# Single-precision 128-point transforms in a bidirectional Hyena and neighbourhood-attention encoder layer

## The chip, the core and the metric

The kernel runs on one NeuronCore of one Trainium2 chip. The core has a matrix engine (TensorE; PE in the profile, with its weight loads as PEld), a vector engine (VectorE, DVE), a scalar engine (ScalarE, ACT), a general engine (GpSimd, POOL) and SyncE (SP), whose queue issues all of this kernel's DMAs. PE reads its operands from the on-chip memory SBUF and adds into the eight banks of PSUM. Each engine works through its own instructions in a fixed order and waits for the others by semaphores. The metric is the time of one execution on the device, in microseconds.

## The reference, cut to what matters

One layer is computed for two sequences, a prompt of 1024 tokens ("p") and a sample of 512 ("s"), of width 1024. Half of the width goes through a Hyena branch, a long convolution by FFT with a filter that a small network makes; the other half goes through attention in windows of a 2-D grid.

```python
h = rmsnorm(x, norm_g);  z = h @ w_in
hy_in = short_conv(hy_in, conv_w, conv_b);  x0, x1, vv = split(hy_in)
kfilt = hyena_filter(L, ...)                       # length 2 L
U = rfft(x1 * vv, n=2 * L);  K = rfft(kfilt, n=2 * L)
y = irfft(U * K, n=2 * L)[:L] + (x1 * vv) * bias
y_hy  = rmsnorm(x0 * y) * silu(hy_gate)
y_att = rmsnorm(neighbourhood_attention(q, k, v, rpb)) * silu(att_gate)
out = x + concat([y_hy, y_att]) @ w_out
```

## The kernel before

**Three products for one.** A float32 product is split: an operand is rounded to fp32r (hi) and the rest kept as a second fp32r tile (lo), and hi*hi + hi*lo + lo*hi are added in PSUM. Projections (L392 and L405), attention and output (L1111) work so, and so do the 128-point transforms. The halves of a weight are made by a cast on ACT or DVE (L365) and a subtraction on POOL (L366).

**The transforms.** A sequence of 2L points is split into classes. DVE makes each class's z, a [128, 2, 128] tile with real and imaginary part (zc), by 8- or 16-point butterflies. Then comes a 128-point transform across the partitions, which is a product with a cosine and a sine matrix of the class. Class 0 holds two real classes and is "packed" (matrices fc); all others are "generic" (matrices dftm). The prompt has 8 classes for each block of 128 channels, the sample has 4, and both have 4 blocks.

In `fwd_generic` ACT casts z into Z (hi, L449), POOL subtracts (lo, L450), and ACT writes the negated copies (L451), so that one row of products serves both parts. `mm3` (L461 to L463) then issues three matmuls of 256 columns for the cosine and three for the sine. `fwd_packed` does the same without the negated copy (L469, L470).

In the filters (`k_phase`, `k_block`) ACT scales the result into Kw, which goes to DRAM. In the convolution (`long_conv`) DVE multiplies the spectrum by the filter's (Kc, from DRAM) into yA and yB, sums them into yA, and ACT, POOL and ACT make Y out of it (L665 to L667) for the inverse transform by `mm3`; ACT copies the result into W, and DVE does the inverse butterflies. The packed class goes through Ybd (L649, L650).

**Constants.** `dft_mats` loads the class matrices as hi and lo, for the filters in one transfer (km), for the prompt's and the sample's convolution each in three, through the room of tiles that are needed later (W, xu, s4). ACT casts them into dftm (L429).

**Stages.** In the first 95 us the prompt's x is normed, turned and split, the filters' network runs, and the first projections start. From 95 to 310 us the filters' transforms alternate with q, k and v of the prompt; from 310 to 575 us there is the prompt's hyena; from 575 to 925 us the prompt's attention runs together with the projections and the hyena of the sample; after that come the outputs and the sample's attention.

**What sets the order.** Generators of each stage are woven in the turns that a plan counts out, with priorities. The framework then lays each engine's instructions in a fixed order from these priorities and an estimate of durations, and waits for a free buffer where a pool has none. `nz`, `nZ`, `nY` and `nK` are the numbers of buffers of z, Z, Y and Kc; yA and yB have nz - 1. The banks for transforms (tag a) are three in the filters, four with b in the prompt's hyena, and one in the sample's.

## Time and profile before

| | |
|---|---|
| Median of 3 runs | 1100.7 us (1096.19 to 1102.8) |
| Span of the profiled execution | 1101.3 us, 18549 instructions |
| PE matmul busy | 1030.7 us (94%), 6492 instructions |
| PE weight loads busy | 895.6 us (81%) |
| DVE busy | 824.4 us (75%), 2098 instructions |
| ACT busy | 561.1 us (51%), 1223 instructions |
| POOL busy | 539.9 us (49%), 480 instructions |
| DMA | 154.87 MB, 141 GB/s over the span |

The profile is one execution, and its own time is its span. Busy shares are means over stages with different limits. A matmul's record covers its whole way through the array, so records of consecutive matmuls overlap, and the price of one is read from the distance of starts. A wait is put down to the semaphore that came last.

### The profile page before, as it was taken

The page shows a single profiled execution, that of the slowest core. Times are in us where ns is not written, and L with a number is a line of the kernel's source. Part 1 is how long each engine was busy: PE and PEld are TensorE (multiplying, and loading weights), DVE is VectorE, ACT ScalarE, POOL GpSimd, SP SyncE. Part 2 cuts the span into 40 slices and gives each one's busy share as a digit, 9 for nine tenths or more (in the row PEclk, how much of TensorE's full clock was granted, in tenths as well). Part 3 has the DMA queues.
Part 4 walks back from the last instruction along what each step waited for, and adds up shares of the span by engine and source line. Part 5 has one row for each costly group of instructions (what it writes and reads, how often), then busy time and mean ns, then how long its engine had stood idle before and what let it go on. Part 6 is the DMA issues. An engine that isn't in the chain of part 4 may idle for free. (4 is left out here: it accounts for less than half of the span.)

```text
span 1101.3 us, 18549 instructions
## 1 busy us (share of the span) xinstructions
PE 1030.7 (94%) x6492; PEld 895.6 (81%) x6492; DVE 824.4 (75%) x2098; ACT 561.1 (51%) x1223; POOL 539.9 (49%) x480
## 2 busy tenths in 40 slices
PE   3999898998999999999898999999999999899998
PEld 2888887987888878787786887888777798798898
DVE  5988679456148597868768898999886868966874
ACT  6644616444534343443425577667567764564530
POOL 2133636325245474545445645455455564766452
PEclk9999999899999999999999899999999999999999
DMA  9134461645612121122375244445544376966522
GB/s 343 34 122 144 143 207 61 219 150 164 224 39 74 46 79 54 50 72 77 118 227 173 78 129 146 120 141 182 140 129 138 114 243 190 321 203 205 164 76 89
DMA packets 110780, 154.87 MB, mean 141 GB/s; under 512 B 7793, under 2 KB 80315, under 8 KB 109919
## 3 DMA queue, kind: packets, MB, share of 16 engines
q1 hardware_dynamic: 110687, 153.69, 44.3%
q8 instruction: 51, 0.84, 0.3%
q14 instruction: 42, 0.34, 0.1%
HBM read 110.35 MB, written 43.32 MB: 140 GB/s over the span
## 5 line engine op out<-in xcount | busy, mean ns | idle before, releaser
L366 POOL TENSOR_TENSOR wlo<-wraw,whi 128x512 fp32r<-128x512 f32 x160 | 231.5, 1451 | 308.4 <-ACT whi L365 180.7
L392 PE MATMUL bank<-hThi_p,whi 128*128 128x512 f32 x320 | 125.2, 391 | 2.0 <-DVE cx L75 2.0
L392 PE MATMUL bank<-hTlo_p,whi 128*128 128x512 f32 x320 | 125.5, 392 | 0.0
L392 PE MATMUL bank<-hThi_p,wlo 128*128 128x512 f32 x320 | 125.4, 392 | 0.0
L405 PE MATMUL bank<-whi,hThi_p 128*128 128x256 f32 x384 | 110.4, 290 | 2.5 <-ACT qsq L849 2.0
L1111 PE MATMUL bank<-whi,hi 128*128 128x256 f32 x384 | 111.0, 291 | 0.8 <-ACT hi L1090 0.5
L405 PE MATMUL bank<-wlo,hThi_p 128*128 128x256 f32 x384 | 110.8, 291 | 0.0
L1111 PE MATMUL bank<-wlo,hi 128*128 128x256 f32 x384 | 110.0, 288 | 0.0
L1111 PE MATMUL bank<-whi,lo 128*128 128x256 f32 x384 | 109.5, 289 | 0.3 <-POOL lo L63 0.3
L405 PE MATMUL bank<-whi,hTlo_p 128*128 128x256 f32 x384 | 108.1, 289 | 0.0
L450 POOL TENSOR_TENSOR Z<-zc,Z 128x256 fp32r<-128x256 f32 x80 | 69.5, 878 | 49.2 <-ACT Z L449 36.2
L1002 ACT ACTIVATE s_sb<-s_sb,mx 128x360 f32<-128x360 f32 (+1 forms) x96 | 60.4, 629 | 63.6 <-DVE mx L998 63.0
L405 PEld LDWEIGHTS bank<-whi,hThi_p 128*128 128x128 f32 x384 | 74.2, 194 | 4.9 <-ACT qsq L849 2.4
L1111 PEld LDWEIGHTS bank<-whi,hi 128*128 128x128 f32 x384 | 73.4, 191 | 4.1 <-issue 2.1
L405 PEld LDWEIGHTS bank<-wlo,hThi_p 128*128 128x128 f32 x384 | 74.5, 194 | 1.6 <-issue 0.7
L1111 PEld LDWEIGHTS bank<-wlo,hi 128*128 128x128 f32 x384 | 73.6, 192 | 1.6 <-issue 1.6
L1111 PEld LDWEIGHTS bank<-whi,lo 128*128 128x128 f32 x384 | 73.1, 192 | 1.7 <-issue 1.1
L405 PEld LDWEIGHTS bank<-whi,hTlo_p 128*128 128x128 f32 x384 | 73.3, 194 | 1.2 <-issue 0.7
L392 PEld LDWEIGHTS bank<-hThi_p,whi 128*128 128x128 f32 x320 | 60.3, 188 | 14.0 <-DVE cx L75 2.4
L392 PEld LDWEIGHTS bank<-hTlo_p,whi 128*128 128x128 f32 x320 | 60.4, 189 | 11.3
L392 PEld LDWEIGHTS bank<-hThi_p,wlo 128*128 128x128 f32 x320 | 60.3, 188 | 11.3
L392 PE MATMUL bank<-hThi_s,whi 128*128 128x512 f32 x160 | 64.6, 407 | 4.4 <-DVE cvv L75 2.3
(292 smaller groups left out, 3108.4 us busy)
## 6 DMA issues: line engine op xcount, KB each, us to landing
wraw<-in_w_ch_dram SPq DMA_DIRECT2D x40, 512.0 KB
wraw<-in_w_tk_dram SPq DMA_DIRECT2D x24, 512.0 KB
wraw<-in_w_out_dram SPq DMA_DIRECT2D x16, 512.0 KB
V<-v_p SPq DMA_DIRECT2D x32, 240.0 KB
v_p<-vg SPq DMA_DIRECT2D x32, 160.0 KB
K_p<-Kw SPq DMA_DIRECT2D x4, 1088.0 KB
x<-in_x_prompt_dram SPq DMA_DIRECT2D x8, 512.0 KB
dec<-in_dec_p_dram SPq DMA_DIRECT2D x16, 256.0 KB
```

The lines of the kernel that those rows point to most:

```text
L366: nc.gpsimd.tensor_tensor(out=lo, in0=r, in1=f32(hi), op=ALU.subtract)
L392: nc.tensor.matmul(ps, lhsT=w, rhs=h[s][:, k], start=(k == 0 and i == 0), stop=(k == KC - 1 and i == 2))
L405: nc.tensor.matmul(pss[t // 2][:, t % 2, :], lhsT=h[t // 4][:, k, t % 4 * P:(t % 4 + 1) * P], rhs=w, start=(k == 0 and i == 0 and t % 2 == ...
L450: nc.gpsimd.tensor_tensor(out=Z[:, 1, 0:2, :], in0=z, in1=f32(Z[:, 0, 0:2, :]), op=ALU.subtract)
L1002: nc.scalar.activation(out=s_sb[:, :n], in_=s_sb[:, :n], func=AF.Exp, bias=mx, scale=-1.0, accum_out=l)
L1111: nc.tensor.matmul(ps[:, j, :], lhsT=h[:, tok], rhs=w, start=(k == 0 and i == 0 and j == 0), stop=(k == 3 and i == 2 and j == 1))
```

## The change

The transforms no longer split their operands. The constants are summed back to single precision (hi + lo, on DVE) when they are loaded, with a third matrix, the negated sine, made by ACT. A generic transform is three matmuls in single precision, straight from zc or yA: one of 256 columns with the cosine and two of 128 columns with the sine and its negative. The packed transform and its inverse are two matmuls of 256 columns each. Z, Y and their conversions on ACT and POOL are gone. Ybd is written by DVE directly, in four half-partition operations instead of two whole ones. The constants come one class at a time, through two tiles in turn (km0, km1 in the filters), four (W, o8, s4, d4) in the prompt's convolution and two (W, s4) in the sample's. In the prompt's hyena `nz` is 8 instead of 4 and `nK` 4 instead of 2. Comments and docstrings were removed as well, so line numbers differ by some 20; they are left out here.

```diff
-        self.fc = g.tile([P, 8, P], F32R, name="fc")
-        m = ["M1f", "M2f", "M1i", "M2i"]
-        self.F = {n: (self.fc[:, 2 * i, :], self.fc[:, 2 * i + 1, :]) for i, n in enumerate(m)}
+        self.fc = g.tile([P, 4, P], F32, name="fc")
+        self.F = {n: self.fc[:, i] for i, n in enumerate(["M1f", "M2f", "M1i", "M2i"])}
...
     def dft_load(self, t, src, pool, tag):
-        r = pool.tile([P, t.shape[1], P], F32, name=tag, bufs=1)
+        r = pool.tile([P, *src.shape[1:]], F32, name=tag, bufs=1)
         self.dma(r, src)
-        self.nc.scalar.copy(out=t, in_=r)
+        self.add(t, r[:, :, 0], r[:, :, 1])
...
     def dft_mats(self, pool, src, fs, stage, tags):
-        t = pool.tile([P, len(fs), 4, P], F32R, name="dftm", bufs=1)
...
+        t = pool.tile([P, len(fs), 3, P], F32, name="dftm", bufs=1)
+        for i, (f, tag) in enumerate(zip(fs, itertools.cycle(tags))):
+            self.dft_load(t[:, i, 0:2], src[:, f - 1].rearrange("p (n a) c -> p n a c", a=2), stage, tag)
+            self.nc.scalar.mul(out=t[:, i, 2], in_=t[:, i, 1], mul=-1.0)
+        return [None] + [tuple(t[:, i, k] for k in range(3)) for i in range(len(fs))]
+    def turn128(self, o, f, z, inverse):
+        c, s, ns = self.dft[f]
+        mm = self.nc.tensor.matmul
+        mm(o, lhsT=c, rhs=z, start=True, stop=False)
+        mm(o[:, 0:P], lhsT=ns if inverse else s, rhs=z[:, 1], start=False, stop=False)
+        mm(o[:, P:], lhsT=s if inverse else ns, rhs=z[:, 0], start=False, stop=True)
...
-    def fwd_generic(self, fp, z, f):
-        Z = fp.tile([P, 2, 3, P], F32R, name="Z", bufs=self.nZ)
-        nc.scalar.copy(out=Z[:, 0, 0:2, :], in_=z)
-        nc.gpsimd.tensor_tensor(out=Z[:, 1, 0:2, :], in0=z, in1=f32(Z[:, 0, 0:2, :]), op=ALU.subtract)
-        nc.scalar.mul(out=Z[:, :, 2, :], in_=f32(Z[:, :, 0, :]), mul=-1.0)
+    def fwd_generic(self, z, f):
         ps = self.bank()
         o = ps[:, 0:256]
-        c, s = self.dft[f]
-        self.mm3(o, c, (Z[:, 0, 0:2, :], Z[:, 1, 0:2, :]), True, False)
-        self.mm3(o, s, (Z[:, 0, 1:3, :], Z[:, 1, 1:3, :]), False, True)
+        self.turn128(o, f, z, False)
...
+    def fwd_packed(self, z):
         ps = self.bank()
-        self.mm3(ps[:, 0:256], self.F["M1f"], (Z[:, 0], Z[:, 1]), True, False)
-        self.mm3(ps[:, 256:512], self.F["M2f"], (Z[:, 0], Z[:, 1]), False, True)
+        for i, n in enumerate(("M1f", "M2f")):
+            self.nc.tensor.matmul(ps[:, i * 256:i * 256 + 256], lhsT=self.F[n], rhs=z, start=i == 0, stop=i == 1)
...
-                self.sub(A[:, 0], A[:, 0], A[:, 1])
-                self.add(A[:, 1], Bt[:, 0], Bt[:, 1])
                 Y = self.Ybd
                 for h in range(2):
                     r = slice(64 * h, 64 * h + 64)
-                    nc.scalar.copy(out=Y[r, 0, :, h, :], in_=A[r])
-                    nc.gpsimd.tensor_tensor(out=Y[r, 1, :, h, :], in0=A[r], in1=f32(Y[r, 0, :, h, :]), op=ALU.subtract)
+                    self.sub(Y[r, 0, h], A[r, 0], A[r, 1])
+                    self.add(Y[r, 1, h], Bt[r, 0], Bt[r, 1])
...
-            Y = fp.tile([P, 2, 3, P], F32R, name="Y", bufs=max(1, self.nY - 1))
-            nc.scalar.copy(out=Y[:, 0, 1:3, :], in_=A)
-            nc.gpsimd.tensor_tensor(out=Y[:, 1, 1:3, :], in0=A, in1=f32(Y[:, 0, 1:3, :]), op=ALU.subtract)
-            nc.scalar.mul(out=Y[:, :, 0, :], in_=f32(Y[:, :, 2, :]), mul=-1.0)
-            c, s = self.dft[f]
-            self.mm3(o, c, (Y[:, 0, 1:3, :], Y[:, 1, 1:3, :]), True, False)
-            self.mm3(o, s, (Y[:, 0, 0:2, :], Y[:, 1, 0:2, :]), False, True)
+            self.turn128(o, f, A, True)
...
-        self.nz, self.nZ, self.nY, self.nK, self.nx, self.nb = 4, 4, 4, 2, 1, 2
-        self.dft = self.dft_mats(fp, self.io["hmat"], range(1, 8), fp, (("W", 4), ("xu", 2), ("s4", 1)))
+        self.nz, self.nZ, self.nY, self.nK, self.nx, self.nb = 8, 4, 4, 4, 1, 2
+        self.dft = self.dft_mats(fp, self.io["hmat"], range(1, 8), fp, ("W", "o8", "s4", "d4"))
...
-        self.dft = self.dft_mats(fp, self.io["hmat"], (2, 4, 6), fp, (("W", 1), ("xu", 1), ("W", 1)))
+        self.dft = self.dft_mats(fp, self.io["hmat"], (2, 4, 6), fp, ("W", "s4"))
```

The framework lays the whole order anew. Three places show how.

On PE, early in the filters, before: the sine products of one class (bank_888) wait for later conversions, so another class and three matmuls of a projection (L405) stand between them.

```order
L461 MATMUL bank_906<-Z_902,dftm_487 128x256
L462 MATMUL bank_888<-Z_884,dftm_487 128x256
L463 MATMUL bank_888<-Z_884,dftm_487 128x256
L405 MATMUL bank_1483<-whi_1181,hThi_p_270 128x256
L405 MATMUL bank_1483<-wlo_1182,hThi_p_270 128x256
L405 MATMUL bank_1483<-whi_1181,hTlo_p_272 128x256
L461 MATMUL bank_888<-Z_884,dftm_487 128x256
L462 MATMUL bank_888<-Z_884,dftm_487 128x256
L463 MATMUL bank_888<-Z_884,dftm_487 128x256
L462 MATMUL bank_906<-Z_902,dftm_487 128x256
L463 MATMUL bank_906<-Z_902,dftm_487 128x256
```

The same place now (L404 is the old L405, L443 to L445 are the three products of `turn128`, L458 the packed one):

```order
L404 MATMUL bank_1037<-whi_1044,hTlo_p_273 128x256
L458 MATMUL bank_891<-zc_888,fc_74 128x256 x2
L443 MATMUL bank_902<-zc_899,dftm_487 128x256
L444 MATMUL bank_902<-zc_899,dftm_487 128x128
L445 MATMUL bank_902<-zc_899,dftm_487 128x128
L443 MATMUL bank_913<-zc_910,dftm_487 128x256
L444 MATMUL bank_913<-zc_910,dftm_487 128x128
L445 MATMUL bank_913<-zc_910,dftm_487 128x128
L404 MATMUL bank_1395<-whi_1146,hThi_p_270 128x256
L404 MATMUL bank_1395<-wlo_1147,hThi_p_270 128x256
```

A class's matmuls now stand together, and read z itself.

On DVE, the same stage, writes of z in the odd classes of the prompt's filters, before, with what they wait for (Pool_49 is POOL's semaphore):

```order
L63 TENSOR_TENSOR zc_952<-oE_946,oO_936 128x256 [waits DVE_49,Pool_49]
L63 TENSOR_TENSOR zc_966<-oE_946,oO_936 128x128 [waits Pool_49]
L63 TENSOR_TENSOR zc_966<-oO_936,oE_946 128x128
L63 TENSOR_TENSOR zc_981<-oE2_947,oO2_937 128x256 [waits DVE_49,Pool_49]
L63 TENSOR_TENSOR zc_995<-oE2_947,oO2_937 128x128 [waits Pool_49]
L63 TENSOR_TENSOR zc_995<-oO2_937,oE2_947 128x128
L850 TENSOR_REDUCE qss8_1282<-qsq_1296 128x8 [waits Activation_49]
```

and now:

```order
L63 TENSOR_TENSOR zc_949<-oE_943,oO_933 128x256 [waits DVE_49,PE_49]
L63 TENSOR_TENSOR zc_956<-oE_943,oO_933 128x128 [waits PE_49]
L63 TENSOR_TENSOR zc_956<-oO_933,oE_943 128x128
L63 TENSOR_TENSOR zc_964<-oE2_944,oO2_934 128x256 [waits DVE_49,PE_49]
L582 MEMSET Kw_879 1x128 [waits Activation_49]
L63 TENSOR_TENSOR oab_1341<-xk_564 128x256 [waits DVE_49]
```

The wait for a free buffer of z moved from POOL to PE; there are 32 such waits for PE at writes of z, all of them in the filters.

Constants of the prompt's convolution, before, on ACT, behind the gates (vg) and ahead of the short convolution (cx1):

```order
L886 ACTIVATE vg_3343<-bank_3318 128x512
L429 CAST dftm_3507<-W_3508 128x2048
L429 CAST dftm_3507<-xu_3511 128x1024
L429 CAST dftm_3507<-s4_3514 128x512
L415 ACTIVATE cx1_3521<-bank_3532,pc_70 128x512
```

and now, on DVE, between the first (vg_2423) and the second half (vg_2750) of v's results (DMAHW are the transfers' semaphores):

```order
L63 TENSOR_TENSOR vg_2423<-bank_2189,vg_2423 128x8x64 [waits DMAHW5_49,DMAHW4_49,DMAHW7_49,DMAHW3_49,Activation_49]
L63 TENSOR_TENSOR dftm_3196<-W_3197 128x256 [waits DMAHW0_49]
L63 TENSOR_TENSOR dftm_3196<-o8_3201 128x256 [waits DMAHW1_49]
L63 TENSOR_TENSOR dftm_3196<-s4_3205 128x256 [waits DMAHW2_49]
L63 TENSOR_TENSOR dftm_3196<-d4_3209 128x256 [waits DMAHW3_49]
L63 TENSOR_TENSOR dftm_3196<-W_3213 128x256 [waits DMAHW0_49]
L63 TENSOR_TENSOR dftm_3196<-o8_3217 128x256 [waits DMAHW1_49]
L63 TENSOR_TENSOR dftm_3196<-s4_3221 128x256 [waits DMAHW2_49]
L63 TENSOR_TENSOR vg_2750<-bank_2534,vg_2750 128x8x64 [waits DMAHW5_49,DMAHW6_49,DMAHW4_49,DMAHW7_49,DVE_49,Activation_49]
```

The load of these constants moved to another engine and ahead of the end of v.

## Rows read from the trace of the kernel before

**Rows 1.** The page's busy shares: us, share of the span, instructions.

```profile
PE 1030.7 (94%) x6492; PEld 895.6 (81%) x6492; DVE 824.4 (75%) x2098; ACT 561.1 (51%) x1223; POOL 539.9 (49%) x480
```

**Rows 2.** Busy us (instructions) by stage: PE, PEld, DVE, ACT, POOL; then clock, DMA.

```profile
95.00:310.00 215.00, 201.39 (x1334) 180.66 (x1333) 127.39 (x348) 99.92 (x253) 94.96 (x86) 0.98 0.48 157
310.00:575.00 265.00, 253.50 (x1341) 215.72 (x1340) 195.33 (x515) 104.76 (x234) 136.80 (x115) 0.98 0.27 85
575.00:925.00 350.00, 336.92 (x2082) 284.11 (x2082) 296.87 (x749) 227.58 (x473) 188.91 (x171) 0.99 0.48 145
```

**Rows 3.** Timeline of PE in the prompt's hyena: start us, us, instruction.

```profile
340.18 0.28 PE L461 MATMUL bank<-Z,dftm 128*128 128x256 f32 x1
...
340.89 0.40 PE L392 MATMUL bank<-hTlo_p,whi 128*128 128x512 f32 x1
```

**Rows 4.** Timeline of PE around a single-precision product of the filters' network.

```profile
52.65 1.02 PE L166 MATMUL bank<-h_s,w 128*128 128x512 f32 x2
53.11 0.68 PE L405 MATMUL bank<-whi,hTlo_p 128*128 128x256 f32 x1
53.63 0.28 PE L405 MATMUL bank<-whi,hThi_p 128*128 128x256 f32 x1
```

**Rows 5.** Chain that ended last: eight single-precision instructions of one column.

```profile
901.76 0.79 PE bank L828 x8
```

**Rows 6.** Costliest groups, conversions: name, forms, count | busy us, mean ns | idle before, releasers.

```profile
L450 POOL TENSOR_TENSOR Z<-zc,Z 128x256 fp32r<-128x256 f32 x80 | 69.5, 878 | 49.2 <-ACT Z L449 36.2 <-issue 6.6 <-DVE vg L63 3.0
...
L451 ACT ACTIVATE Z<-Z 128x256 fp32r<-128x256 f32 x80 | 33.1, 417 | 39.5 <-POOL Z L450 39.2
L449 ACT CAST Z<-zc 128x256 fp32r<-128x256 f32 x80 | 31.2, 403 | 19.7 <-DVE zc L75 7.9 <-DVE zc L63 6.1 <-PE bank L463 3.3
```

**Rows 7.** The same view, matmuls of the transforms, with most idle time before them.

```profile
L462 PE MATMUL bank<-Z,dftm 128*128 128x256 f32 x160 | 46.4, 292 | 4.7 <-POOL Z L450 4.7
L461 PE MATMUL bank<-Z,dftm 128*128 128x256 f32 x160 | 46.2, 291 | 3.3 <-DVE yB L63 1.2 <-ACT Kw L600 0.8 <-ACT Z L451 0.6
...
L461 PE MATMUL bank<-Z,fc 128*128 128x256 f32 x32 | 9.4, 292 | 2.6 <-ACT Z L469 2.6
```

**Rows 8.** The same view, weight loads of the transforms.

```profile
L462 PEld LDWEIGHTS bank<-Z,dftm 128*128 128x128 f32 x160 | 30.9, 193 | 6.9 <-POOL Z L450 5.9
L461 PEld LDWEIGHTS bank<-Z,dftm 128*128 128x128 f32 x160 | 30.7, 192 | 6.2 <-issue 1.7 <-ACT Kw L600 1.2 <-ACT Z L451 0.9
...
L461 PEld LDWEIGHTS bank<-Y,dftm 128*128 128x128 f32 x80 | 15.2, 191 | 4.7 <-ACT Y L665 3.1 <-issue 0.2 <-ACT ya L1033 0.2
...
L461 PEld LDWEIGHTS bank<-Z,fc 128*128 128x128 f32 x32 | 6.2, 193 | 3.3 <-ACT Z L469 2.8
```

**Rows 9.** The same view, three operations of DVE.

```profile
L63 DVE TENSOR_TENSOR yA<-yB 128x128 f32<-128x128 f32 x48 | 20.4, 435 | 0.7
...
L63 DVE TENSOR_TENSOR yA<-bank,Kc 128x256 f32<-128x256 f32 x40 | 16.7, 419 | 7.8 <-DMA Kc<-K_p 2.4 <-POOL Y L666 2.0 <-POOL Ybd L650 1.7
...
L63 DVE TENSOR_TENSOR zc<-oE,oO 128x256 f32<-128x256 f32 x16 | 12.6, 789 | 1.3 <-POOL Z L470 1.3
```

**Rows 10.** Instructions on z: count, ns least/median/most, first and last start, forms.

```profile
L63 DVE TENSOR_TENSOR zc<-oE,oO x32: 273/411/2605, 104.1 to 523.1; 128x256 f32<-128x256 f32 x16, 128x128 f32<-128x128 f32 x16
```

**Rows 11.** Waits of PE outside the transforms: us in total, times, longest us.

```profile
PE bank L405 <- POOL wlo L366: 3.9, 2, 2.8
PE bank L271 <- DVE px L79: 3.4, 2, 1.9
PE bank L945 <- DVE mx L998: 2.8, 3, 1.4
PE bank L392 <- DVE cvv L75: 2.3, 1, 2.3
```

**Rows 12.** Busy time of the engines while the first projections run.

```profile
20.00:95.00 75.00, 72.31 (x512) 63.21 (x511) 67.64 (x157) 41.25 (x69) 14.53 (x12) 1.00 0.37 127
```

**Rows 13.** Costliest groups: a cast of the sample's constants on ACT.

```profile
L429 ACT CAST dftm<-W 128x512 fp32r<-128x512 f32 x2 | 1.2, 620 | 5.7 <-DMA W<-in_hmat_dram 5.7
```

More of the change, by code (lines that the diff above doesn't have):

```diff
@@ L425, in dft_load @@
     def dft_load(self, t, src, pool, tag):
-        r = pool.tile([P, t.shape[1], P], F32, name=tag, bufs=1)
+        r = pool.tile([P, *src.shape[1:]], F32, name=tag, bufs=1)
         self.dma(r, src)
-        self.nc.scalar.copy(out=t, in_=r)
+        self.add(t, r[:, :, 0], r[:, :, 1])
     def dft_mats(self, pool, src, fs, stage, tags):
-        t = pool.tile([P, len(fs), 4, P], F32R, name="dftm", bufs=1)
-        step, i = fs[1] - fs[0], 0
-        for tag, n in tags:
-            if step == 1:
-                self.dft_load(t[:, i:i + n].rearrange("p f a c -> p (f a) c"),
-                              src[:, fs[i] - 1:fs[i] - 1 + n].rearrange("p f a c -> p (f a) c"), stage, tag)
-            else:
-                self.dft_load(t[:, i], src[:, fs[i] - 1], stage, tag)
-            i += n
@@ L443, in dft_mats @@
-        return [None] + [((t[:, i, 0], t[:, i, 1]), (t[:, i, 2], t[:, i, 3])) for i in range(len(fs))]
-    def fwd_generic(self, fp, z, f):
-        nc = self.nc
-        Z = fp.tile([P, 2, 3, P], F32R, name="Z", bufs=self.nZ)
-        nc.scalar.copy(out=Z[:, 0, 0:2, :], in_=z)
-        nc.gpsimd.tensor_tensor(out=Z[:, 1, 0:2, :], in0=z, in1=f32(Z[:, 0, 0:2, :]), op=ALU.subtract)
-        nc.scalar.mul(out=Z[:, :, 2, :], in_=f32(Z[:, :, 0, :]), mul=-1.0)
+        t = pool.tile([P, len(fs), 3, P], F32, name="dftm", bufs=1)
@@ L452, in fwd_generic @@
+    def fwd_generic(self, z, f):
         ps = self.bank()
         o = ps[:, 0:256]
-        c, s = self.dft[f]
-        self.mm3(o, c, (Z[:, 0, 0:2, :], Z[:, 1, 0:2, :]), True, False)
-        self.mm3(o, s, (Z[:, 0, 1:3, :], Z[:, 1, 1:3, :]), False, True)
+        self.turn128(o, f, z, False)
         return o.rearrange("p (a c) -> p a c", a=2), ps[:, 256:512]
-    def mm3(self, out, Ls, Rs, first, last):
-        nc = self.nc
-        nc.tensor.matmul(out, lhsT=Ls[0], rhs=Rs[0], start=first, stop=False)
-        nc.tensor.matmul(out, lhsT=Ls[0], rhs=Rs[1], start=False, stop=False)
-        nc.tensor.matmul(out, lhsT=Ls[1], rhs=Rs[0], start=False, stop=last)
@@ L465, in fwd_packed @@
-    def fwd_packed(self, fp, z):
-        nc = self.nc
-        Z = fp.tile([P, 2, 3, P], F32R, name="Z", bufs=self.nZ)[:, :, 0:2, :]
-        nc.scalar.copy(out=Z[:, 0], in_=z)
-        nc.gpsimd.tensor_tensor(out=Z[:, 1], in0=z, in1=f32(Z[:, 0]), op=ALU.subtract)
+    def fwd_packed(self, z):
         ps = self.bank()
-        self.mm3(ps[:, 0:256], self.F["M1f"], (Z[:, 0], Z[:, 1]), True, False)
-        self.mm3(ps[:, 256:512], self.F["M2f"], (Z[:, 0], Z[:, 1]), False, True)
+        for i, n in enumerate(("M1f", "M2f")):
+            self.nc.tensor.matmul(ps[:, i * 256:i * 256 + 256], lhsT=self.F[n], rhs=z, start=i == 0, stop=i == 1)
@@ L772, in hyena @@
         sqs = cp.tile([P, L], F32, name="sqs", bufs=1)
-        self.Ybd = fp.tile([P, 2, 2, 2, P], F32R, name="Ybd", bufs=1)
-        nc.gpsimd.memset(f32(self.Ybd), 0.0)
+        self.Ybd = fp.tile([P, 2, 2, P], F32, name="Ybd", bufs=1)
+        nc.gpsimd.memset(self.Ybd, 0.0)
         def front(blk):
@@ L1188, in run @@
         self.w3_load(mp)
[L1189 to L1190 removed]
+        self.dft_load(self.fc, self.io["fconst"].rearrange("p (n a) c -> p n a c", a=2), sp, "fc")
+        self.dft = self.dft_mats(kd, self.io["kmat"], range(1, 8), sp, ("km0", "km1"))
         cls(mc, sc, xc)
```

14 lines of the change are left out of this document (6 added, 8 removed).

## Prediction, made before the changed kernel ran

> **What bounds the kernel now.** I first read the busy shares: TensorE (PE) is busy for 1030.7 of 1101.3 us, DVE for 824, POOL for 540 and ACT for 561 [rows 1]. That figure alone proves little, since a matmul's record is longer than the time it takes from the next one. The stages say more. In the three that hold the transforms, PE is busy for 201 of 215 us, 254 of 265 and 337 of 350; DVE comes near it only in the third, with 297 of 350 [rows 2]. So PE is the bound nearly everywhere, DVE is second in the third stage, and what the change does to PE's own queue counts first.
>
> The spacing of starts gives the true price of a matmul. In the prompt's hyena a group of six transform matmuls starts at 340.18, and the projection behind it begins at 340.89 [rows 3]: 0.71 us for a group of six, or 0.118 us for each of 256 columns, although each record says 0.28.
>
> **The change part by part.**
>
> PE's work. A transform of one class is a group of six such matmuls. The code makes 48 groups in the filters, 64 in the prompt's hyena and 32 in the sample's, which is 144 groups and 864 matmuls. At 0.71 us they take 102 us. Afterwards a group streams 512 columns in single precision: 256 and twice 128 for an ordinary class, twice 256 for the packed class and its inverse. The kernel already has one single-precision product, the 512-column one of the filters' layers. The profile shows it as two instructions. From its start at 52.65 to the second matmul behind it at 53.63 are 0.98 us, and 0.12 of that is the matmul in between [rows 4], so 512 columns cost 0.86 us. That is 0.15 a group over the old 0.71: 144 x 0.15 = 22 us. It is the lower end. The new pieces are small, though: an ordinary class becomes six instructions, four of them 128 columns wide, each with a weight load. The sums over tokens have single-precision instructions with one column only, and eight of them take 0.79 us [rows 5], so no instruction with its load comes under about 0.10 us. By the 0.86 us, 128 columns need 0.107, close to that floor, and the 256-column products took 0.118 for the same kind of pair. If every narrow piece costs 0.12 and every wide one 0.225, a group costs 0.93 and the whole 31 us. I take 0.18 a group, 26 us. Some of this falls where DVE holds PE back anyway: of the 32 groups in the third stage I count half, so 3 us are hidden. **PE: +23 us, between +18 and +31.** The forecast rests on this term, since PE has almost nothing else to do in that time.
>
> The conversions. Before each group ACT rounds z (0.40 us), POOL subtracts (0.88), and ACT writes the negated copy (0.42): 1.7 us in a row, and the same before each inverse [rows 6]. All of that goes; PE then waits for DVE's z alone. What it is worth is what PE idles there. In the three largest of the twelve kinds of transform matmul the records show 4.7, 3.3 and 2.6 us, 10.6 together [rows 7]; these see only gaps longer than a record's overhang. The weight loads, which are shorter, show 6.9, 6.2, 4.7 and 3.3, or 21.1 us [rows 8]. Most releasers there are ACT and POOL. Not all of it is gained: the order on PE now puts a group right behind DVE's z, so that a late z stalls PE where a late conversion did before. **Conversions: -16 us, between -5 (half of 10.6) and -21.**
>
> The relief of POOL and DVE. POOL loses 69.5 us in one of the four subtractions [rows 6], and ACT its casts. DVE gains too. A 128x256 product with one operand in PSUM takes 419 ns; a sum of the same size with both in SBUF takes 789, and a 128x128 one takes 435 [rows 9], more than half the price of twice its size. The row of all z's written from two tiles shows 273 at best and 2605 at worst [rows 10]. The trace thus has DVE waiting within instructions while POOL works. The Trainium skill, in the page SBUF — State Buffer, section Who interferes with whom, says why: a DVE instruction with two SBUF inputs and a GpSimd instruction that reads SBUF exclude one another, and one with a single SBUF input is free of it. The trace agrees, with 419 against 789 ns. PE's largest waits for POOL's weight halves and for DVE, outside the transforms and after the start, are 3.9, 3.4, 2.8 and 2.3, or 12.4 us [rows 11]. POOL keeps the weight halves, which are its largest work, so I give half of these. **Relief: -6 us, between 0 and -12.**
>
> What DVE gets in return. The constants were cast by ACT; now DVE adds high and low: 17 classes of 256 columns and one of 512, at 0.42 to 0.79 us [rows 9], 7 to 14 us in all, and 16 more half-tile operations in the packed inverse, up to 7 us. Eight of the sums fall into the first 95 us, in which DVE is busy for 67.6 of the 75 us from 20 us on [rows 12] and makes the low halves that PE waits for. Seven stand in DVE's queue between the results of v, each behind its own transfer. ACT waited 5.7 us for such transfers in the sample [rows 13]; now DVE waits, and behind it stand v's results, which free PE's banks. PE has the second half of v in its banks by then, 192 matmuls of 0.12 us or 23 us, so a wait of some 6 us is covered there. If that cover is gone, it is 6 us. The three constants of the sample come where DVE is second to PE, and there little covers them. **Constants: +3 us, between 0 and +8.** More buffers for K spare a wait of 2.4 us on K's transfer [rows 9]; I count it at nothing, since PE is not late there. Eight buffers for z in the prompt's hyena replace four for z and four for Z: nothing.
>
> **The sum:** 23 - 16 - 6 + 3 = +4 on 1101.3 us, so 1105 in that execution. It lies 0.6 above the median of the runs shown, 1100.7, which I leave in the rounding: 1105.
>
> **The rivals.**
>
> *PE gains more than it pays (faster).* Every transform stall goes (-21), the relief is at its bound (-12), and DVE's unblocking gives another 5 in the third stage, where it is busy for 297 of 350 us; the constants cost nothing, PE pays 23: -15, so 1086. It rests on the exclusion of DVE and POOL: POOL's four subtractions end, and DVE stops being late with z. For it speaks that the profile shows POOL and ACT as releasers of most transform stalls; against it, that the weight halves stay and that z now has no stage behind it.
>
> *z is held by PE (slower).* Before, a z was free as soon as POOL had subtracted; now it is free when PE, in its own order, has read it. In the filters 32 of DVE's writes of z wait for PE, with four buffers where there were four and three. While DVE waits, the sums of squares, the results of v and the turned x behind it wait too, and then PE does. At 0.5 us a wait that is 16 us, and with the forecast's +4, less what the wait costs nothing (about 1), 1120. From 0.2 us a wait, 7 us in all, the kernel is over 1% slower. DVE is busy for only 127 of 215 us in that stage [rows 2], which speaks against it.
>
> *Single precision at the old rate* would save work instead of adding it. The 0.86 us of [rows 4] excludes it.
>
> **How the numbers follow.** The forecast, 1105 with 1094 to 1116 as its own range, gets 0.50, the faster rival 0.22, the slower one 0.28. A measurement of this kernel can tell about 1%, so faster is below 1089.7 and slower above 1111.7. Faster: 0.18 of the first rival and 0.03 of the forecast. Slower: 0.24 of the second and 0.06 of the forecast. The rest, 0.49, is the same. The sum's own bounds reach from 18 - 21 - 12 + 0 = -15 to 31 - 5 - 0 + 8 = +34, but they will hardly all fall on one side; from 1085 to 1124, about 1 in 10 is left out at either end.
>
> **What would show each step.** Start to start, an ordinary transform group of six instructions should take 0.86 to 0.93 us; at 0.71 or less the first term is wrong, and the kernel is faster. Idle time before transform matmuls should be under a third of [rows 7, 8], with DVE as the releaser. A 128x256 sum on DVE with both operands in SBUF should come under 789 ns. If DVE shows waits for PE at z in the filters, the slower rival is at work; if the stage from 575 us on shrinks by more than 5 us, the faster one is.

## The result, and the profile after

The changed kernel takes 1112.2 us (1110.0 to 1115.4) against 1100.2 (1096.2 to 1102.8) for the kernel before: 1.0115 times, with a 95% interval of 1.0088 to 1.0142. The forecast was 1105 (1085 to 1124): the time lies in its range, 7 us above its value, and just beyond the 1% that a measurement can tell. The profiled execution took 1110.0, with a span of 1108.3.

The busy shares, beside [rows 1]:

```profile
PE 1047.0 (94%) x6444; PEld 910.8 (82%) x6444; DVE 798.4 (72%) x2132; ACT 464.0 (42%) x958; POOL 409.5 (37%) x328
```

POOL has lost 130 us, ACT 97, DVE 26, and PE has gained 16. Busy time by stage, the stretches and columns of [rows 2], with the first one ahead of them:

```profile
0.00:95.00 95.00, 72.58 (x469) 62.29 (x470) 76.40 (x167) 46.75 (x84) 19.52 (x22) 0.96 0.49 166
95.00:310.00 215.00, 205.37 (x1342) 184.33 (x1341) 118.41 (x369) 73.26 (x175) 47.14 (x37) 0.99 0.49 160
310.00:575.00 265.00, 261.15 (x1357) 223.84 (x1355) 184.68 (x547) 65.35 (x117) 84.53 (x51) 1.00 0.30 92
575.00:925.00 350.00, 335.19 (x1996) 281.54 (x1997) 297.18 (x756) 196.34 (x399) 155.64 (x128) 0.98 0.47 139
```

In the prompt's hyena (310 to 575) PE is idle for only 4 us, where it was idle for 11.5 [rows 2]. POOL and ACT are busy for less in each of these four stretches, POOL in the first by only 0.7 us.

PE in the prompt's hyena, where several groups follow one another (start us, us): the three products of one, and the first of the next:

```profile
353.01 0.60 PE L443 MATMUL bank<-zc,dftm 128*128 128x256 f32 x2
353.45 0.39 PE L444 MATMUL bank<-zc,dftm 128*128 128x128 f32 x2
353.67 0.39 PE L445 MATMUL bank<-zc,dftm 128*128 128x128 f32 x2
353.89 0.60 PE L443 MATMUL bank<-zc,dftm 128*128 128x256 f32 x2
```

A group takes 0.88 us from start to start, against 0.71 [rows 3]: 0.44 for 256 columns and 0.22 for each 128. The Trainium skill, in the page FP8 and Floating Point Precision, section TensorE Precision Notes, says that true single precision makes four passes through the array; against three products that gives an estimate of four thirds. The trace here shows less, 0.88 to 0.71, or 1.24.

The idle time before the transforms, first the matmuls that have any, as in [rows 7], then the largest of the weight loads, as in [rows 8]:

```profile
L443 PE MATMUL bank<-zc,dftm 128*128 128x256 f32 x160 | 47.9, 381 | 0.1
...
L636 PE MATMUL bank<-Ybd,fc 128*128 128x256 f32 x16 | 5.0, 392 | 1.8 <-DVE Ybd L63 1.8
```

```profile
L444 PEld LDWEIGHTS bank<-zc,dftm 128*128 128x128 f32 x160 | 30.2, 189 | 4.2
...
L636 PEld LDWEIGHTS bank<-Ybd,fc 128*128 128x128 f32 x16 | 2.6, 189 | 2.7 <-issue 1.4 <-PE bank L391 1.1
```

The matmuls' 10.6 us of [rows 7] have become 1.9. The four largest gaps before weight loads, 21.1 us in [rows 8], are 10.9 (4.2 and 2.7 are shown, 2.1 and 1.9 stand before other rows), so half remains. POOL is no longer named before either, and ACT only with 0.3 us for Kw and 0.2 for raw. What PE waits for now is something else. Its largest waits outside the transforms and after the start (us in total, times, longest), beside [rows 11]:

```profile
PE bank L404 <- DVE vg L63: 6.0, 3, 2.4
PE bank L391 <- DVE vg L63: 5.9, 4, 2.7
```

The tile vg is where v's results wait for their store. Before, PE's wait for DVE at vg was 0.4 us in all. The chain of work that ended last shows the same place (start us, us; its longest pieces): from 230 to 289 us it runs through one store of v after another, at 259 us through a load of Kc between two of them, and PE comes back only behind them.

```profile
230.44 3.81 DMA v_p<-vg
238.17 3.86 DMA v_p<-vg
245.85 5.55 DMA v_p<-vg
258.97 3.43 DMA Kc<-K_p
264.57 4.00 DMA v_p<-vg
271.48 3.51 DMA v_p<-vg
277.91 4.38 DMA v_p<-vg
285.16 3.54 DMA v_p<-vg
290.81 33.18 PE bank L391 x145
324.86 11.80 PE bank L391 x52
```

Why this chain lies bare is seen in the filters. The rows of the tile Kw, which takes their results, first in the kernel before, then after (count: ns least/median/most, first to last start):

```profile
L600 ACT ACTIVATE Kw<-bank x40: 363/384/454, 101.9 to 282.4; 128x256 f32<-128x256 f32 x40
```

```profile
L585 ACT ACTIVATE Kw<-bank x40: 363/383/447, 102.6 to 242.7; 128x256 f32<-128x256 f32 x40
```

The transforms of the filters used to run until 282 us, beside the stores of v (its eight results were written from 213 to 272 us). Without conversions they are done by 243, while v's results now come from 226 to 282. From 245 us on, PE has only the second half of v's products and, from 263 us, the projections of the hyena to do beside the stores, and both need banks that v's results still hold.

Last, the start. DVE scales the second half of x at 37.85 us in the kernel before, and here at:

```profile
45.70 2.73 DVE L79 TENSOR_SCALAR x<-x,rs_y 128x1024 f32<-128x1024 f32 x4
```

The eight sums of constants, from 25.40 to 40.1 us, stand ahead of it. PE waits for its input twice, and from 44.7 to 51.5 us it is granted the lower of its two clocks, 1.2 instead of 2.4 GHz (start us, us, idle before and its releaser; then 20 to 60 us by engine, with the mean granted clock of 0.91 behind the busy times):

```profile
43.47 1.12 PE L165 MATMUL bank<-h_p,w 128*128 128x512 f32 x2 [1.90 <-ACT h_p L179]
46.59 2.80 PE L247 MATMUL bank<-ident,x 128*128 128x128 f32 x12 [1.99 <-DVE x L79]
```

```profile
20.00:60.00 40.00, 35.76 (x220) 29.88 (x219) 38.04 (x82) 20.90 (x38) 1.58 (x2) 0.91 0.26 88
```

Before, 284 matmuls were done in that stretch at a clock of 1.00; here 220.

So three candidates stood for the 12 us: PE's price for single precision, the sums on DVE at the start, and v's stores. The runs were chosen to tell these apart, and then to check the two halves of the gain. Ratios are to the kernel before, measured again beside each run, so that they say more than the times.

| run | us | ratio (95%) |
|---|---|---|
| changed kernel | 1112.2 | 1.0115 (1.0088 to 1.0142) |
| sums of the start on POOL | 1111.2 | 1.0101 (1.0065 to 1.0136) |
| sums of hyena on POOL | 1114.3 | 1.0121 (1.0086 to 1.0156) |
| old buffers | 1112.9 | 1.0123 (1.0095 to 1.0150) |
| no split, old price | 1092.8 | 0.9931 (0.9911 to 0.9951) |
| one product | 1087.2 | 0.9887 (0.9857 to 0.9918) |
| two vg | 1102.6 | 1.0018 (0.9997 to 1.0040) |
| two vg, all sums on POOL | 1104.8 | 1.0039 (1.0019 to 1.0060) |
| no split, two vg | 1082.6 | 0.9858 (0.9826 to 0.9889) |
| one product, two vg | 1073.6 | 0.9775 (0.9748 to 0.9801) |
| before, two tiles for v | 1097.6 | 0.9977 (0.9956 to 0.9998) |
| spare POOL work | 1131.9 | 1.0279 (1.0250 to 1.0308) |
| no split, two vg, spare POOL work | 1118.2 | 1.0165 (1.0147 to 1.0183) |

In the text below, a hundredth of a ratio is 11 us.

### The profile page after: what moved, and what is told of

Read it like the earlier page. It is cut to its first block, busy times and chain, and to the rows that moved or that the text cites. A ratio compares the mean times of both kernels' runs of the same rounds, so it can differ in the third digit from the quotient of the medians.

```text
span 1108.3 us, 18053 instructions
## 1 busy us (share of the span) xinstructions
PE 1047.0 (94%) x6444; PEld 910.8 (82%) x6444; DVE 798.4 (72%) x2132; ACT 464.0 (42%) x958; POOL 409.5 (37%) x328
## 4 chain that ended last, share of the span: by engine, by line
PE 64%; DVE 16%; DMA 11%; ACT 3%; SPq 3%; issue 2%; POOL 1%; DVEq 0%; ACTq 0%; POOLq 0%
PE bank L391 23%; PE bank L404 10%; PE bank L1088 8%; PE bank L443 3%; PE bank L1006 3%; DMA v_p<-vg 3%; SPq L60 3%; PE bank L997 2%; PE bank L972 2%; PE bank L445 2%; PE bank L444 2%; DMA v_s<-vg 2%; DVE rs_t L63 1%; PE bank L554 1%; PE bank L971 1%
## 5 line engine op out<-in xcount | busy, mean ns | idle before, releaser
L365 POOL TENSOR_TENSOR wlo<-wraw,whi 128x512 fp32r<-128x512 f32 x160 | 230.7, 1445 | 525.4 <-ACT whi L364 338.6
L404 PE MATMUL bank<-whi,hThi_p 128*128 128x256 f32 x384 | 112.3, 294 | 4.2 <-DVE vg L63 3.6
L404 PE MATMUL bank<-wlo,hThi_p 128*128 128x256 f32 x384 | 111.5, 292 | 0.0
L404 PE MATMUL bank<-whi,hTlo_p 128*128 128x256 f32 x384 | 109.4, 292 | 0.0
L364 ACT CAST whi<-wraw 128x512 fp32r<-128x512 f32 x66 | 40.8, 622 | 111.3 <-PE bank L391 68.6
L404 PEld LDWEIGHTS bank<-whi,hThi_p 128*128 128x128 f32 x384 | 75.0, 196 | 6.6 <-DVE vg L63 4.0
L404 PEld LDWEIGHTS bank<-wlo,hThi_p 128*128 128x128 f32 x384 | 75.0, 195 | 1.6 <-issue 1.0
L404 PEld LDWEIGHTS bank<-whi,hTlo_p 128*128 128x128 f32 x384 | 73.4, 194 | 1.8 <-issue 0.5
L364 DVE CAST whi<-wraw 128x512 fp32r<-128x512 f32 x94 | 56.1, 600 | 25.4 <-issue 4.9
L1006 PE MATMUL bank<-pt,V 120*64 120x256 f32 (+1 forms) x352 | 67.3, 297 | 2.8 <-DVE pt L63 2.3
```

What stands on the lines that cost most here:

```text
L364: next(self.w_round)(out=hi, in_=r)
L365: nc.gpsimd.tensor_tensor(out=lo, in0=r, in1=f32(hi), op=ALU.subtract)
L404: nc.tensor.matmul(pss[t // 2][:, t % 2, :], lhsT=h[t // 4][:, k, t % 4 * P:(t % 4 + 1) * P], rhs=w, start=(k == 0 and i == 0 and t % 2 == ...
L1006: nc.tensor.matmul(o, lhsT=vl, rhs=pr_, start=(c == 0 and i == 0), stop=(c == ncu - 1 and i == 1))
```

## The experiments

**The sums of the start on POOL.** `dft_load` and `dft_mats` hand the engine on to the addition.

```diff
-        self.dft_load(self.fc, ..., sp, "fc")
+        self.dft_load(self.fc, ..., sp, "fc", self.nc.gpsimd)
-        self.dft = self.dft_mats(kd, self.io["kmat"], range(1, 8), sp, ("km0", "km1"))
+        self.dft = self.dft_mats(kd, self.io["kmat"], range(1, 8), sp, ("km0", "km1"), self.nc.gpsimd)
```

> The eight sums of high and low constants in the first stage (fc and the filters' seven classes) run on POOL instead of DVE; nothing else is changed. Theory A (the sums stand in DVE's queue ahead of the normalisation of the prompt's second half, which PE's transposes wait for; in the trace after, that row starts at 45.70 us against 37.85 before, and PE idles and falls to half clock from 44.6 to 51.5 us): the row comes back to 37 to 40 us, the half-clock stretch goes, and the kernel gains 5 to 8 us, to 1104 to 1107. Theory B (eight sums of 0.34 to 0.67 us are 3 us of DVE and are covered; the loss is elsewhere): within 2 us of the changed kernel, 1110 to 1114.

Theory A is half right, and its time is wrong. The mechanism is there: DVE's row comes back to 40.23 us, and PE does 266 matmuls from 20 to 60 us at full clock. But the kernel gains nothing that can be measured. Its 1111.2 us lie in theory B's range, within an interval of some 4 us either way. The stretches from 20 to 60 us and from 80 to 100 us show where the gain goes:

```profile
20.00:60.00 40.00, 37.47 (x266) 32.24 (x265) 38.46 (x78) 24.26 (x45) 11.16 (x11) 1.00 0.31 101
80.00:100.00 20.00, 17.41 (x114) 15.64 (x114) 15.56 (x38) 5.83 (x13) 6.65 (x6) 0.92 0.47 153
```

From 80 to 100 us PE now waits (2.6 us for ACT's squares of q), has a mean granted clock of 0.92 and does 114 matmuls, where the changed kernel does 139 at 1.00. Over the first 100 us that leaves 15 of the 46 that had been won. And v's first result comes at 225.3 us, where it came at 225.8. The loss at the start was real, but a later wait takes most of what is won there, and by v's first result all but 0.5 us is gone. The sums also cost POOL time that they had cost DVE, so the run shows what the move is worth, not the sums alone.

**The sums of the convolution's constants on POOL.**

```diff
-        self.dft = self.dft_mats(fp, self.io["hmat"], range(1, 8), fp, ("W", "o8", "s4", "d4"))
+        self.dft = self.dft_mats(fp, self.io["hmat"], range(1, 8), fp, ("W", "o8", "s4", "d4"), self.nc.gpsimd)
```

The sample's three classes are changed in the same way.

> The changed kernel with the sums of the convolution's constants (seven classes for the prompt, three for the sample) on POOL instead of DVE; those of the first stage stay on DVE. In the trace after, DVE waits 9.6 us for these transfers with v's results behind them in its queue. Theory A (DVE's wait holds v's banks): 2 to 6 us faster than the changed kernel, 1106 to 1110. Theory B (v's results wait for their own stores in any case, and those transfers only share the queue): 1110 to 1115.

Theory B. DVE no longer waits for these transfers (POOL does, 16.4 us), and PE's waits for vg stay: 4.2 and 7.2 us, where they were 6.0 and 5.9. So it is not DVE's queue that holds v.

**The old buffer counts in the prompt's hyena.**

```diff
-        self.nz, self.nZ, self.nY, self.nK, self.nx, self.nb = 8, 4, 4, 4, 1, 2
+        self.nz, self.nZ, self.nY, self.nK, self.nx, self.nb = 4, 4, 4, 2, 1, 2
```

> The changed kernel with the buffer counts of before in the prompt's hyena: four for z and two for K instead of eight and four. The forecast's step said that these buffers are worth nothing: 1109 to 1115. A rival (z is held by PE, so that buffers carry the gain in the stage from 310 to 575 us, where the changed kernel stalls 7 us less): 1117 or more.

1112.9: the buffers are worth nothing that shows, as forecast. The other half of that rival is seen in the changed kernel's trace. Its filters have four buffers for z. This is all the idle time of DVE ahead of its writes of z that PE ended (us, times):

```profile
  PE bank L445: 0.9, 2
```

**Two tiles for v's results.**

```diff
-                vh = tp.tile([P, 2, 4, P], F32R, name="vg", bufs=1)
+                vh = tp.tile([P, 2, 4, P], F32R, name="vg", bufs=self.nvg)
```

with nvg 2 until the prompt's hyena is done, then 1, and the same for the gates and the squares that share the tile.

> The changed kernel with two buffers instead of one for vg, the tile in which v's results (and the gates) wait for their store, in the prompt's first stage and hyena; in the trace after, the eight results of v are written at 225.8 to 282.4 us, 6.4 to 10.3 us apart, each waiting for the store of the one before, while all of the filters' transforms are done by 240 us. Theory A (the end of the filters' stage is set by this chain of stores, so neither the 6 us lost at the start nor PE's price there counts): PE's waits on vg go (3.6 and 4.5 us before 575 us), the chain is shorter, and the kernel gains 5 to 12 us: 1100 to 1107. Theory B (PE's own work sets that end, the waits are covered): 1109 to 1114.

Theory A: 0.0097 of the ratio, or 10.7 us, come back, nearly all that the change had lost. ACT's writes of v in the changed kernel, the first four (start us, us, idle before):

```profile
225.76 0.59 ACT L846 CAST vg<-bank 128x512 fp32r<-128x512 f32 x1 [0.87 <-PE bank L404]
234.41 0.59 ACT L846 CAST vg<-bank 128x512 fp32r<-128x512 f32 x1 [1.81 <-DMA v_p<-vg]
242.20 0.58 ACT L846 CAST vg<-bank 128x512 fp32r<-128x512 f32 x1 [1.86 <-DMA v_p<-vg]
251.50 0.58 ACT L846 CAST vg<-bank 128x512 fp32r<-128x512 f32 x1 [8.43 <-DMA v_p<-vg]
```

and with two tiles:

```profile
225.01 0.59 ACT L846 CAST vg<-bank 128x512 fp32r<-128x512 f32 x1 [0.87 <-PE bank L404]
225.75 0.59 ACT L846 CAST vg<-bank 128x512 fp32r<-128x512 f32 x1
233.28 0.59 ACT L846 CAST vg<-bank 128x512 fp32r<-128x512 f32 x1 [1.43 <-DMA v_p<-vg]
237.58 0.59 ACT L846 CAST vg<-bank 128x512 fp32r<-128x512 f32 x1 [3.43 <-DMA v_p<-vg]
```

The four are out by 238 instead of 252 us. They free the banks that the second half of v and the hyena's projections behind it need, and the last result of v is written at 270.4 instead of 282.4. The chain that ended last now runs through PE alone in this place:

```profile
262.45 54.66 PE bank L391 x241
317.98 11.80 PE bank L391 x52
```

The same 52 matmuls began at 324.86 in the changed kernel. The two profiled executions differ by 6.9 us in all (1108.3 and 1101.4), and this is the distance here already: all of it arises by then.

**The same in the kernel before.** Here every second result goes to a second tile in the room of raw:

```diff
+                if alt and m % 2:
+                    vh = alt.tile([P, 2, 4, P], F32R, name=f"raw{nt}", bufs=1)
+                else:
+                    vh = tp.tile([P, 2, 4, P], F32R, name="vg", bufs=1)
```

> The kernel before, with every second result of v in the prompt written to a second tile (the room of raw, which is free by then), so that a store no longer holds the next result. It asks whether the chain of v's stores bound the kernel before too. Theory A (before, the filters' transforms were late, ran until 278 us and filled PE beside the chain; only the change uncovered it): 1097 to 1103. Theory B (the chain costs both kernels the same): 1089 to 1094.

Theory A, with at most a small gain: 0.9977, or 2.5 us (0.2 to 4.8). Its last result of v is also out earlier, at 259 instead of 272 us, but the filters' transforms run until 281 us all the same. The chain of stores became a cost mainly through the change. That the filters' transforms are what had covered it is read from these times; no run moved them alone.

**All sums on POOL, and two vg in both groups.** The edits of the first two runs and of the one with two tiles together, and nvg stays 2 for the sample:

```diff
-        self.dft = self.dft_mats(fp, self.io["hmat"], (2, 4, 6), fp, ("W", "s4"))
+        self.dft = self.dft_mats(fp, self.io["hmat"], (2, 4, 6), fp, ("W", "s4"), self.nc.gpsimd)
```

> The changed kernel with all sums of constants on POOL and two buffers for vg in both groups: what the two causes are worth together. Theory A (once v's chain of stores no longer sets the end of the first stage, the 6 us that the sums cost at the start come out as well): 1093 to 1102. Theory B (PE is the bound, and these waits are covered): 1108 to 1114.

Theory A fails: 1104.8 us, between the two ranges, and with 1.0039 no better than two vg alone (1.0018). With the stores out of the way, what is won at the start still doesn't come out at the end. That the sums cost 3 us, as the forecast had it, can't be seen in any run; 0 fits better.

**No split, at the old price.** The change without single precision: six rounded matmuls a group, as before, on what DVE writes; z, yA, Ybd, fc and dftm are rounded tiles, and the packed products are likewise made three times.

```diff
-        mm(o, lhsT=c, rhs=z, start=True, stop=False)
-        mm(o[:, 0:P], lhsT=ns if inverse else s, rhs=z[:, 1], start=False, stop=False)
-        mm(o[:, P:], lhsT=s if inverse else ns, rhs=z[:, 0], start=False, stop=True)
+        for i in range(3):
+            mm(o, lhsT=c, rhs=z, start=i == 0, stop=False)
+        for i in range(3):
+            mm(o, lhsT=ns if inverse else s, rhs=z, start=False, stop=i == 2)
```

> The changed kernel, but each transform is again six matmuls of 256 columns in the rounded form at the old price (0.71 us a group), now fed by DVE's z directly: no conversion by ACT or POOL comes before them. Left out are the low halves and the signs, so only the time counts. Against the changed kernel it takes away single precision's price alone, against the kernel before it takes away the conversions (and adds the sums of constants). Theory A (PE is the bound, single precision costs it 0.17 us in each of 144 groups): 24 us faster than the changed kernel, 1083 to 1093. Theory B (PE's extra time lies where DVE or the transfers of v hold it anyway): 1100 or more.

It lies in theory A's range, at its upper edge: 1.0115 less 0.9931 is 0.0184, or 20 us, for single precision alone. But against the kernel before only 0.0069, 7.6 us, come from all that was taken off ACT and POOL. The same kernel with two vg, by the edit above:

> The kernel without split (six rounded matmuls of 256 columns a group at the old price, no conversions; low halves and signs left out) with two buffers for vg in the prompt's part. Against the kernel before it shows what the conversions, POOL's relief and the sums of constants are worth together once v's chain of stores is out of the way; the forecast's terms were -16, -6 and +3, so -19. Theory A (the chain gave 10 us of them back): 1080 to 1086. Theory B (the chain binds only with single precision's longer groups): 1089 to 1094. The distance to the changed kernel with two vg (1102.6) is PE's price without that cover, 17 to 24 us by the forecast.

With two vg, 0.9858: theory A again. The conversions, the relief and the sums are worth 15.6 us together, and the single tile for v had taken half of that back. Against the kernel before with two tiles for v (0.9977), which is the closer pair, they are worth 0.0119, or 13 us. From here to the changed kernel with two vg, 0.9858 to 1.0018, single precision costs 17.6 us.

**One product.** The changed kernel's own three matmuls, on rounded operands.

```diff
-        z = fp.tile([P, 2, P], F32, name="zc", bufs=self.nz)
+        z = fp.tile([P, 2, P], F32R, name="zc", bufs=self.nz)
```

and the same for yA, Ybd, fc and dftm.

> The changed kernel with its own matmuls (256 and twice 128 columns) on operands that DVE writes rounded, one product each: half the instructions. The low parts are left out, so only the time counts. By the old price of 0.118 us for 256 columns a group costs 0.34 us instead of 0.88. Theory A (PE is the bound throughout): most of 144 x 0.54 = 78 us comes back, 1035 to 1060. Theory B (a second bound, DVE or the transfers of v, lies closely under PE): 1075 or more.

The price of a group is as estimated. PE in the prompt's hyena, 0.34 us from group to group, and the weight loads of the same stretch, 0.11 us from start to start:

```profile
344.91 0.33 PE L443 MATMUL bank<-zc,dftm 128*128 128x256 f32 x1
345.08 0.22 PE L444 MATMUL bank<-zc,dftm 128*128 128x128 f32 x1
345.14 0.28 PE L445 MATMUL bank<-zc,dftm 128*128 128x128 f32 x1
345.25 0.33 PE L443 MATMUL bank<-zc,dftm 128*128 128x256 f32 x1
```

```profile
345.08 0.19 PEld L445 LDWEIGHTS bank<-zc,dftm 128*128 128x128 f32 x1
345.19 0.19 PEld L443 LDWEIGHTS bank<-zc,dftm 128*128 128x128 f32 x1
345.30 0.19 PEld L444 LDWEIGHTS bank<-zc,dftm 128*128 128x128 f32 x1
```

The matmuls' own starts lie 0.17, 0.06 and 0.11 us apart, and it is their sum that counts. At 0.118 us for 256 columns, 512 columns alone would take 0.24; the group takes three times 0.11, so each instruction with its load costs the same here, whether it has 256 columns or 128.

Yet against the changed kernel 0.0228, or 25 us, are gained of the 78 that PE no longer has to do. Theory A is refuted. PE is the bound only to a small depth: take away more, and two things show in its place. One is waiting: PE idles for 95 us of the span (1084.3 less 989.3), where it idled for 61. Here are the two largest waits behind the start (us in total, times, longest):

```profile
PE bank L391 <- DVE vg L63: 9.3, 4, 3.2
PE bank L270 <- DVE px L79: 7.9, 1, 7.9
```

The other is the clock. Behind the wait of 7.9 us, the granted clock is 0.71 from 180 to 200 us, where it was 1.00. The columns of [rows 2] show it for two of the stages, beside 0.99 and 1.00 in the changed kernel:

```profile
95.00:310.00 215.00, 196.18 (x1244) 174.74 (x1244) 122.60 (x373) 74.52 (x179) 52.80 (x40) 0.94 0.50 162
310.00:575.00 265.00, 243.62 (x1226) 205.80 (x1225) 199.86 (x592) 70.45 (x127) 92.80 (x60) 0.97 0.32 101
```

Over the whole span the mean is 0.958 instead of 0.985. With two levels, of which the lower is half the other, that is by estimate 91 us at the lower one instead of 33, which can take up to 29 us of PE's work at full clock. The 34 us of idle time and these together are enough for the 53 us that did not come back.

The same with two vg:

> The kernel with one rounded product (0.34 us a group by the old price; low halves left out) and two buffers for vg in the prompt's part, as the fastest version that these runs point to. Theory A (v's chain binds the first stage): 6 to 10 us faster than with one vg (1087.2), 1077 to 1081. Theory B (with so little PE work the stage is bound by DVE or by v's own sums): 1084 or more.

1073.6, faster than expected: here the second vg is worth 0.0112, or 12 us. Against the changed kernel with two vg, 27 us of the 78 come back. This is the fastest version of all, 2.25% under the kernel before, at the price of the low halves in the transforms. Of the versions in full single precision, the changed kernel with two vg is the best, and it is level with the kernel before.

**Spare work on POOL.** What was the relief worth? The subtractions are put back, with no reader, also ahead of the packed transforms and of the inverses.

```diff
+    def spare(self, z):
+        self.sub(self.sp_out, z, self.fc[:, 0:2], self.nc.gpsimd)
...
+        self.spare(z)
         ps = self.bank()
```

> The changed kernel with 136 spare subtractions of 128x256 on POOL, one ahead of each transform of a class and one ahead of each inverse, as before; each reads z (or the product) and constants, and nobody reads what it writes. ACT's two conversions are not put back, and PE waits for none of it. Theory A (relief of DVE from POOL is worth the 6 us of the forecast, up to 12): 1118 to 1124. Theory B (DVE's longer instructions lie under PE's longer matmuls): 1110 to 1115. Where z is held longer, DVE's waits for POOL at z show it.

1.0279, more than theory A asked for: the spare work costs 18 us, where the forecast's bound for the relief was 12. The sum of two tiles of [rows 9], first in the changed kernel, then here, and the busy shares here:

```profile
L63 DVE TENSOR_TENSOR zc<-oE,oO 128x256 f32<-128x256 f32 x16 | 7.4, 460 | 0.0
```

```profile
L63 DVE TENSOR_TENSOR zc<-oE,oO 128x256 f32<-128x256 f32 x16 | 11.1, 694 | 0.0
```

```profile
PE 1055.8 (93%) x6444; PEld 916.6 (81%) x6444; DVE 846.0 (75%) x2132; ACT 463.7 (41%) x958; POOL 522.7 (46%) x464
```

DVE does the same instructions in 846 us instead of 798. It waits for POOL to release z for only 0.7 us, so it is not z that is held: its own instructions are longer, 789 ns before, 460 after, 694 here. This is what the Trainium skill's page SBUF — State Buffer, section Who interferes with whom, states of two SBUF inputs on DVE and reads of GpSimd; the three means agree with it. Not every sum follows: the 128x128 one into yA of [rows 9], on which the prediction leaned too, takes 435 ns before, 434 after and 449 here.

The same spare work in the kernel without split, with two vg:

> The kernel without split and with two buffers for vg (1082.6 us), with the 136 spare subtractions on POOL put back, whose results nobody reads. PE's work is that of the kernel before, PE waits for no conversion, but DVE again shares its time with POOL. It splits the 16 to 17 us that conversions and relief are worth together. Theory A (nearly all of it is the relief of DVE from POOL; the conversions' own length was hidden): 1096 to 1102, as before. Theory B (the forecast's split: the conversions held PE by their length, 16 us, and POOL's work costs DVE's customers 6 us): 1086 to 1091.

1.0165, beyond both theories: 34 us slower than without the spare work, and 18 us slower than the kernel before, which has the real conversions. DVE is busy for 837 us, against 800 without. So the spare work costs more than the whole gain from taking the conversions away, and it can't be the relief turned round.

The trace says where it costs. The matmuls on hThi_p in the prompt's hyena start from 279.7 to 554.7 us here, and from 251.8 to 525.4 without the spare work. So 28 of the 38 us between the two profiled executions (1116.5 and 1078.9) are lost ahead of the hyena, with 48 of the spare subtractions, and only 1.4 us in the prompt's hyena, with 60 of them. In the changed kernel too, 15 of 22 us are lost ahead of it (278.6 against 263.5). Part of the loss is not DVE's: PE waits 4.6 us for a weight half from POOL, and the mean granted clock is 0.967 instead of 0.983, by estimate 37 us more at the lower level, or up to 18 us of work.

How the 13 to 16 us divide into relief and the conversions' own length is thus not shown. Why the kernel before bears its POOL work so much better stays open. It has its transforms later in PE's order, so that a late z need not hold PE; that would explain it, but no run tested it.

## Why the prediction was right, and where it was not

The time lies in the range of the forecast's own case (1094 to 1116). It is 1.15% above the kernel before, where the likeliest class was the same (0.49) and slower had 0.30; by the prediction's own bound of 1111.7 it is slower, by half a microsecond. One term was missing, two were too large in opposite directions and cancel, and the split of one of them was not borne out. That the sum without the missing term comes out so close is in part luck.

- **PE's price: right.** 0.88 us a group, in the range of 0.86 to 0.93, and 0.17 more than before. On the kernel it is 17.6 us (two vg) to 20 us (one), where the step said 23, between 18 and 31, so at the lower end. The floor of about 0.10 us for an instruction with its load, on which the upper end rested, is borne out: 0.11 for 128 columns in the rounded form. In single precision a product of 128 columns is two instructions and takes 0.22, so the narrow pieces stand at that floor and cost nothing extra by it.
- **Conversions, relief and constants: -19 forecast, -15.6 measured** once v has two tiles, and -13 against the kernel before with two tiles as well. The sum is right to 3 to 6 us; its parts are not shown. The conversions were given -16 and the relief -6, by what PE's waits named as releasers: POOL's Z and ACT's Z [rows 7, 8]. The spare work costs 18 us in the changed kernel and 34 without split, so POOL's work can cost far more than the 12 that the step allowed, most of it in the filters; but as 34 is more than the whole gain, it does not measure the relief. The step took the waits for POOL's weight halves and for DVE [rows 11] as all that POOL's reading could cost, and left out that z itself can be late through DVE's long instructions. The constants' +3 is not seen in any run; the nearest value is 0.
- **Without v's stores the sum was +4; the kernel with two vg stands at +2**, or at +4.5 against the kernel before with two tiles. In that pair PE costs 5 us less than forecast, and the other terms bring 6 us less.
- **The missing term: +8 to +11 us for v's stores** (10.7, less the 2.5 that two tiles bring to the kernel before). The step that failed is the one on the constants: "PE has the second half of v in its banks by then, 192 matmuls of 0.12 us or 23 us, so a wait of some 6 us is covered there." It named the place and the price if the cover is gone, and took the wrong thing as the cover and the wrong thing as the wait. By the traces the cover was the filters' transforms, which ended at 282 us and now end at 243, and at 242 to 250 in every run without conversions and without spare work; and the wait is not for the constants (moving them changes nothing) but for a store that has one tile. The earlier transforms thus took PE's work away from the place that needed it. No row of before showed that wait (0.4 us); it could have been read from the writes of v, each behind the store of the one before, and from asking what PE does meanwhile.
- **"z is held by PE": refuted**, with 0.9 us of waits and no loss from the old buffer counts. The time went toward that rival, by another mechanism.
- **"PE gains more than it pays": its mechanism is at work**, as DVE's sum at 460 instead of 789 ns and the spare work show; its time failed by the stores, and since the gain (13 to 16 us) is less than what PE pays (18 to 20).
- **What was to show each step** came as said in two places, the group's 0.88 us and DVE's sum at 460 ns, and half in a third: before matmuls the idle time is 1.9 us of 10.6, with DVE as the releaser, but before weight loads 10.9 of 21.1, most of it without a releaser. The stage from 575 us on shows none of the faster rival's gain: DVE is busy there for 297 us, as before [rows 2], and the sample's projections, the matmuls on hThi_s, start at 547 us in both kernels and end at 892 instead of 879.
- **"What bounds the kernel now": too strong.** PE's added 24 us came through to three quarters, but of 78 us taken away only 25 to 27 came back, the rest going to waits and to a lower granted clock.

## What to carry to other kernels

When a change lets work start earlier, ask what that work was covering where it stood: a chain of stores through one tile cost little here (2.5 us) while the bound engine had something else to do, and 10.7 us when that work had moved ahead. Here a busy share near 95% gave the price of added work, but not the gain from removed work: behind it stood waits, and a clock that falls after them. And a releaser named before a stall (a conversion on POOL) can itself slow the engine ahead of it. Putting its work back without a reader shows that it does; how much of a gain that was, it tells only where the order around it stays the same.

## What the runs showed of the hardware

In the rounded form a matmul of 256 columns with its own weight load costs PE 0.12 us from start to start, and 128 columns cost hardly less: where groups of 256, 128 and 128 follow one another, each takes 0.34 us, and their loads start 0.11 apart. In single precision 256 columns cost 0.44 and 128 cost 0.22, each as two instructions with a load each. And 136 subtractions on POOL, of 0.72 us at the least, lengthen DVE's instructions by 36 to 48 us in all (837 against 800 us, 846 against 798), with hardly any wait that the profile names (0.7 us for z): it shows in the mean duration of DVE's operations with two inputs in SBUF, such as 694 against 460 ns for a sum of 128x256.
